# Folding the adaLN sums in place, and moving each unit's first scaling to ScalarE

## The chip, the core and the metric

The kernel runs on one core of a Trainium2 chip. It is measured by the device time of one execution in microseconds; lower is better. Five engines work side by side, each through its own queue in order, and wait for each other by semaphores: TensorE (PE; its weight loads are shown apart as PEld), VectorE (DVE), ScalarE (ACT), GpSimd (POOL) and SyncE (SP), which here only issues DMAs.

## The reference: what is computed

One inference step through two layers of a diffusion backbone on 384 tokens (128 of context, 256 latent). Each layer is a half-step SwiGLU FFN, a mixer of four head groups, and a second FFN. Every sub-layer's input is normalised and then scaled, shifted and gated by nine vectors that come from a conditioning vector:

```
mod_ctx = (jax.nn.silu(c_ctx) @ w_ada[l] + b_ada[l]).reshape(1, N_MOD, -1)
mod_lat = (jax.nn.silu(c) @ w_ada[l] + b_ada[l]).reshape(c.shape[0], N_MOD, -1)
h = rmsnorm(x, p['g_ff1']) * (1 + part(1)) + part(0)
x = x + 0.5 * part(2) * swiglu(h, p['w1_gate'], p['w1_up'], p['w1_down'])
```

`w_ada[l]` is 1024 x 9216, so for each layer the kernel has to multiply two vectors (context and latent) with a matrix of 36 MB. These two products are the adaLN sums.

## The kernel before, in words

**FFN.** The weights come in pieces of 128 x 1024 by SP's DMAs. Each piece is split in two: ScalarE rounds it to `hi` (L243), VectorE takes the rest as `lo` (L244), and TensorE makes three products of each block (L248 to L250), each with a 128x128 stationary block and 384 moving columns. The first half of an FFN (`gate_up`) makes the hidden rows `sg`, which ScalarE and VectorE finish (L567, L568) and split into `ah`, `al` (L253, L254); the second half multiplies them with the down weights into `pd`.

**The adaLN sums** run beside three of the four FFNs. The plan cuts the columns of `w_ada` that the start does not compute into 43 units (42 of three column tiles of 128, one of two). A unit (`ada_steps`) loads its 128 x 8 x 384 weights into `flat`. With the 1024 inputs as 8 groups `k` of 128 partitions, it builds for each of the two streams `s` a partial sum per partition in `acc[:, s, :]`: the first scaling writes it (L276), seven more add to it (L278, multiply and add). Then the sum over the 128 partitions is left, `ada_reduce`:

```
298  nc.gpsimd.dma_start(out=fold[0:64, :c], in_=acc[64:128, 0, :c])
299  nc.gpsimd.dma_start(out=fold[64:128, :c], in_=acc[0:64, 1, :c])
302  G.tensor_tensor(out=fold[h, :c], in0=acc[h, s, :c], in1=fold[h, :c], op=ALU.add)
308  T.transpose(pt[:, m * P:(m + 1) * P], fold[:, m * P:(m + 1) * P], ident)
310  S.activation(out=junk[:, 0:64], in_=pt[:, m * 64:(m + 1) * 64], func=AF.Identity, accum_out=pm[:, m:m + 1])
```

Two transfers fold one half of the partitions of each stream onto the other, two POOL additions add them, TensorE transposes the three tiles, and ScalarE sums the columns by six accumulating activations. `ada_finish` (L268, L269) adds the bias and multiplies by the gain into `mod`.

**What sets the order.** `Filler` gives the units out in steps. Each piece of an FFN's weights earns it a number of credits (`up(2 * ru)`, `dn(rd)`), at a rate of 8 steps a unit; one credit is one `k` of the unit at work. A finished unit's reduction is started at once (its transfers and POOL additions), and its TensorE part is given out six steps later (`late`, `flush`). Two units are loaded at a time, and `acc` has two buffers. Within this the framework's scheduler, which has a cost model of its own, sets each engine's order; the mixer's attention part is scheduled by hand and has no units.

Of the kernel before, what the change touches and what calls it, by code (L numbers as in the profile page):

```python
# [9 lines left out]
F32 = mybir.dt.float32  # L10
# [3 lines left out]
AF = mybir.ActivationFunctionType  # L14
ALU = mybir.AluOpType
AX = mybir.AxisListType

P = 128
DM = 1024
KD = DM // P  # L20
# [70 lines left out]
def trunk_kernel(ctx: ExitStack, tc: tile.TileContext, I: dict, C: dict, O: list):  # L91
    nc = tc.nc
    V, S, G, T = nc.vector, nc.scalar, nc.gpsimd, nc.tensor
# [7 lines left out]
    sm = ctx.enter_context(tc.tile_pool(name="sm", bufs=2))  # L101
# [7 lines left out]
    def small(name):  # L109
        return psm.tile([P, 512], F32, tag="sm", name=name)  # L110
# [4 lines left out]
    def cload(name, shape, src, pool=None, eng=None):  # L115
        t = (pool or const).tile(shape, F32, name=name)
        (eng or nc.gpsimd).dma_start(out=t, in_=src)
        return t
# [46 lines left out]
    ident = cload("ident", [P, P], C["ident"], eng=nc.scalar)  # L165
    cols_b0 = columns("b0", [("b_ada0", row128(I["b_ada"][0:1]), 72, nc.scalar), ("g_ff1", row128(I["g_ff1"]), 16, nc.scalar)])
    ones = const.tile([P, P], F32, name="ones")
    V.memset(ones, 1.0)
    sc = const.tile([P, KD, 2], F32, name="sc")
# [88 lines left out]
    junk = const.tile([P, P], F32, name="junk")  # L258
# [4 lines left out]
    def ada_load(w, l, kt, n):  # L263
        nc.sync.dma_start(out=w, in_=I["w_ada"][l][:, kt * P:(kt + n) * P].rearrange("(k p) f -> p k f", p=P))

    def ada_finish(l, kt, n, sums):
        mp = mod[:, l, kt:kt + n, :]
        V.tensor_tensor(out=mp, in0=sums.rearrange("p (k s) -> p k s", s=2), in1=bc(badd[:, l, kt:kt + n].unsqueeze(2), [P, n, 2]), op=ALU.add)  # L268
        V.tensor_tensor(out=mp, in0=mp, in1=bc(bmul[:, l, kt:kt + n].unsqueeze(2), [P, n, 2]), op=ALU.mult)  # L269

    last_step = [None]

    def ada_product(acc, w, n, k):
        for s in range(2):
            if k == 0:
                last_step[0] = V.tensor_scalar(out=acc[:, s, :n * P], in0=w[:, 0, :], scalar1=sc[:, 0, s:s + 1], scalar2=None, op0=ALU.mult)  # L276
            else:
                last_step[0] = V.scalar_tensor_tensor(out=acc[:, s, :n * P], in0=w[:, k, :], scalar=sc[:, k, s:s + 1], in1=acc[:, s, :n * P], op0=ALU.mult, op1=ALU.add)  # L278

    def ada_acc():  # L280
        return sm.tile([P, 2, 3 * P], F32, tag="adacc", bufs=2, name="adacc")
# [12 lines left out]

    def ada_reduce(acc, l, kt, n):
        c = n * P
        fold = sm.tile([P, 3 * P], F32, tag="adfold", bufs=1, name="adfold")
        nc.gpsimd.dma_start(out=fold[0:64, :c], in_=acc[64:128, 0, :c])  # L298
        nc.gpsimd.dma_start(out=fold[64:128, :c], in_=acc[0:64, 1, :c])
        for s in range(2):  # L300
            h = slice(64 * s, 64 * s + 64)
            G.tensor_tensor(out=fold[h, :c], in0=acc[h, s, :c], in1=fold[h, :c], op=ALU.add)  # L302

        yield False
        pm = sm.tile([P, 6], F32, tag="adasum", bufs=2, name="adasum")
        pt = small(f"ada{l}_{kt}")
        for m in range(n):
            T.transpose(pt[:, m * P:(m + 1) * P], fold[:, m * P:(m + 1) * P], ident)
        for m in range(2 * n):
            S.activation(out=junk[:, 0:64], in_=pt[:, m * 64:(m + 1) * 64], func=AF.Identity, accum_out=pm[:, m:m + 1])  # L310
        ada_finish(l, kt, n, pm[:, :2 * n])

    def ada_steps(l, kt, n, stage):

        w = stage(n)
        ada_load(w, l, kt, n)
        yield True
        acc = ada_acc()
        for k in range(KD):
            ada_product(acc, w, n, k)  # L320
            if k < KD - 1:
                yield True
        red = ada_reduce(acc, l, kt, n)
        next(red)
        yield red
# [12 lines left out]
    class Filler:  # L338
# [1 line left out]
        late = []  # L340

        def __init__(self, units, stage):
            self.units, self.stage, self.run, self.credit = list(units), stage, [], 0.0

        def start(self):
            if self.units:
                g = ada_steps(*self.units.pop(0), self.stage)
                next(g)
                self.run.append(g)

        def __call__(self, steps):
            self.credit += steps
            while self.credit >= 1.0 and (self.run or self.units):
                self.credit -= 1.0
                while len(self.run) < 2 and self.units:
                    self.start()
                red = next(self.run[0])
                if red is not True:
                    self.run.pop(0)
                    self.late.append([6, red])  # L360
                self.flush(1)

        def flush(self, steps):
            for t in list(self.late):
                t[0] -= steps
                if t[0] < 0:
                    self.late.remove(t)
                    with tc.issue_after(last_step[0].ins):
                        next(t[1], None)

        def begin(self):
            for _ in range(2):
# [1301 lines left out]
```

## Time and profile before

| | us |
|---|---|
| median of 3 runs | 1611.67 (1611.38 to 1614.06) |
| the profiled execution | 1614.9 |
| its span, first to last instruction | 1613.1 |
| PE busy | 1561.6 (97%) |
| DVE busy | 1245.8 (77%) |
| ACT busy | 786.8 (49%) |
| POOL busy | 255.4 (16%) |

A busy time is the sum of an engine's instructions. Products overlap in TensorE's pipeline: one lasts 0.34 us, while the next starts 0.17 us after it. What a product costs is therefore read from the distance of starts, and not from its length. An f32 product (not fp32r, as the FFN's are) is recorded as two passes, each with its own weight load, so three products show as x6.

### The profile page before, as it was taken

Reading aid. Unit: us, or ns where it says so; the run is one execution under the profiler, and the core shown is the slowest. Engines: PE = TensorE matmul, PEld = TensorE weight load, DVE = VectorE, ACT = ScalarE, POOL = GpSimd, SP = SyncE. Lnnn points to the kernel's source line nnn. Section 1 sums busy time; section 2 is a strip of 40 time slices with the busy share of each in tenths; the row PEclk is TensorE's granted clock in tenths of the full one; section 3 lists DMA queues with packets and bytes.
Section 4 is the critical chain, followed back from the end, with each engine's and each line's share of the span. In section 5 each row is a group of like instructions: output and inputs, shape, how many; then the busy total and the mean of one; then the engine's idle time right before and its main releaser. Section 6 shows DMA issues by size and latency. Waiting matters only on the chain. (4 is left out here: it accounts for less than half of the span.)

```text
span 1613.1 us, 24761 instructions
## 1 busy us (share of the span) xinstructions
PE 1561.6 (97%) x9027; PEld 1467.4 (91%) x9027; DVE 1245.8 (77%) x2485; ACT 786.8 (49%) x1838; POOL 255.4 (16%) x334
## 2 busy tenths in 40 slices
PE   7899999999999999999999999999999999999997
PEld 5789989997867999999999999999886799999997
DVE  5799997997878699996999977698787767434333
ACT  5544434548465554444546344454846656333332
POOL 2112221232040001131220212123004000000000
PEclk9999999999999999999999999999999999999999
DMA  9757758664432367867676865675344234444341
GB/s 309 247 151 232 225 185 247 208 199 120 121 75 75 109 204 232 253 179 222 212 206 192 250 195 164 213 231 158 116 111 86 66 110 126 122 126 131 118 137 46
DMA packets 233375, 270.68 MB, mean 168 GB/s; under 512 B 12392, under 2 KB 217936, under 8 KB 233253
## 3 DMA queue, kind: packets, MB, share of 16 engines
q1 hardware_dynamic: 223232, 248.67, 50.8%
q0 software_dynamic: 9744, 20.31, 5.3%
q8 instruction: 71, 1.16, 0.3%
q14 instruction: 52, 0.42, 0.1%
q10 hardware_dynamic: 276, 0.11, 0.0%
HBM read 257.10 MB, written 3.57 MB: 162 GB/s over the span
## 5 line engine op out<-in xcount | busy, mean ns | idle before, releaser
L278 DVE SCALAR_TENSOR_TENSOR adacc<-flat,sc,adacc 128x384 f32<-128x384 f32 (+1 forms) x602 | 357.2, 646 | 0.0
L302 POOL TENSOR_TENSOR adfold<-adacc,adfold 64x384 f32<-64x384 f32 (+1 forms) x86 | 118.0, 1372 | 174.7 <-DMA adfold<-adacc 172.3
L253 ACT CAST ah<-sg 128x384 fp32r<-128x384 f32 x88 | 45.1, 513 | 163.1 <-DVE sg L568 162.3
L250 PE MATMUL pd<-ah,lo_db 128*128 128x384 f32 x352 | 118.8, 338 | 1.6 <-DVE lo_db L244 1.4
L250 PE MATMUL pd<-ah,lo_da 128*128 128x384 f32 x352 | 118.7, 337 | 1.6 <-DVE lo_da L244 1.6
L249 PE MATMUL pg<-wide,hi_gb 128*128 128x384 f32 (+1 forms) x352 | 119.3, 339 | 0.2
L248 PE MATMUL pd<-ah,hi_da 128*128 128x384 f32 x352 | 119.3, 339 | 0.0
L248 PE MATMUL pg<-wide,hi_gb 128*128 128x384 f32 (+1 forms) x352 | 119.2, 339 | 0.0
L248 PE MATMUL pd<-ah,hi_db 128*128 128x384 f32 x352 | 118.9, 338 | 0.0
L250 PE MATMUL pg<-wide,lo_gb 128*128 128x384 f32 (+1 forms) x352 | 118.5, 337 | 0.0
L249 PE MATMUL pu<-wide,hi_ub 128*128 128x384 f32 (+1 forms) x352 | 118.4, 336 | 0.0
L249 PE MATMUL pd<-al,hi_db 128*128 128x384 f32 x352 | 118.4, 336 | 0.0
L249 PE MATMUL pd<-al,hi_da 128*128 128x384 f32 x352 | 118.4, 336 | 0.0
L248 PE MATMUL pu<-wide,hi_ub 128*128 128x384 f32 (+1 forms) x352 | 118.2, 337 | 0.0
L250 PE MATMUL pu<-wide,lo_ub 128*128 128x384 f32 (+1 forms) x352 | 117.8, 337 | 0.0
L248 PE MATMUL pu<-wide,hi_ua 128*128 128x384 f32 (+1 forms) x328 | 111.3, 340 | 4.2 <-DVE sg L568 4.2
L250 PE MATMUL pg<-wide,lo_ga 128*128 128x384 f32 (+1 forms) x328 | 112.0, 343 | 1.9 <-DVE lo_ga L244 1.9
L248 PE MATMUL pg<-wide,hi_ga 128*128 128x384 f32 (+1 forms) x328 | 113.5, 346 | 0.0
L249 PE MATMUL pg<-wide,hi_ga 128*128 128x384 f32 (+1 forms) x328 | 112.0, 342 | 0.0
L298 POOL DMA_DIRECT2D adfold<-adacc x43 | 23.9, 556 | 550.5 <-DVE adacc L278 352.0
L249 PE MATMUL pu<-wide,hi_ua 128*128 128x384 f32 (+1 forms) x328 | 110.9, 338 | 0.0
L250 PE MATMUL pu<-wide,lo_ua 128*128 128x384 f32 (+1 forms) x328 | 110.6, 338 | 0.0
(504 smaller groups left out, 4290.9 us busy)
## 6 DMA issues: line engine op xcount, KB each, us to landing
flat<-in_w_ada_dram SPq DMA_DIRECT2D x42, 1536.0 KB, 8.1
st_gb<-in_w_gate_dram SPq DMA_DIRECT2D x44, 512.0 KB, 3.8
st_ub<-in_w_up_dram SPq DMA_DIRECT2D x44, 512.0 KB, 4.5
st_ga<-in_w_gate_dram SPq DMA_DIRECT2D x41, 512.0 KB, 3.9
st_ua<-in_w_up_dram SPq DMA_DIRECT2D x41, 512.0 KB, 4.9
st_da<-in_w_down_dram SPq DMA_DIRECT2D x40, 512.0 KB, 4.8
st_db<-in_w_down_dram SPq DMA_DIRECT2D x40, 512.0 KB, 3.5
wst<-in_w_ada_dram SPq DMA_DIRECT2D x8, 1024.0 KB, 12.6
```

The lines of the kernel that those rows point to most:

```text
L248: T.matmul(out, lhsT=lh, rhs=rh, start=start, stop=False)
L249: T.matmul(out, lhsT=lh, rhs=rl, start=False, stop=False)
L250: T.matmul(out, lhsT=ll, rhs=rh, start=False, stop=stop)
L253: S.copy(hi, src)
L278: last_step[0] = V.scalar_tensor_tensor(out=acc[:, s, :n * P], in0=w[:, k, :], scalar=sc[:, k, s:s + 1], in1=acc[:, s, :n * P], op0=ALU.mu ...
L298: nc.gpsimd.dma_start(out=fold[0:64, :c], in_=acc[64:128, 0, :c])
L302: G.tensor_tensor(out=fold[h, :c], in0=acc[h, s, :c], in1=fold[h, :c], op=ALU.add)
```

## The change

Four things are done, and the order of instructions follows from them.

- The two fold transfers add into `acc` itself (`accum_op`), so that `acc[0:64, 0]` and `acc[64:128, 1]` hold what `fold` held. The POOL additions and `fold` go.
- The sum over the remaining 64 partitions is made by products with a column of ones: for each stream and each tile one f32 product with a 64x128 stationary block and one moving column, six a unit, in place of three transposes. Two small copies take the results, in place of six accumulating activations. `ada_finish` comes two steps later.
- The first scaling (`k = 0`) goes from VectorE to ScalarE.
- It is given out a step ahead, when the unit before is done (`primed`), so that a unit takes seven credits and not eight.

```
     def ada_product(acc, w, n, k):
         for s in range(2):
             if k == 0:
-                last_step[0] = V.tensor_scalar(out=acc[:, s, :n * P], in0=w[:, 0, :], scalar1=sc[:, 0, s:s + 1], scalar2=None, op0=ALU.mult)
+                S.activation(out=acc[:, s, :n * P], in_=w[:, 0, :], func=AF.Identity, scale=sc[:, 0, s:s + 1])
...
         c = n * P
-        fold = sm.tile([P, 3 * P], F32, tag="adfold", bufs=1, name="adfold")
-        nc.gpsimd.dma_start(out=fold[0:64, :c], in_=acc[64:128, 0, :c])
-        nc.gpsimd.dma_start(out=fold[64:128, :c], in_=acc[0:64, 1, :c])
+        nc.gpsimd.dma_start(out=acc[0:64, 0, :c], in_=acc[64:128, 0, :c], accum_op=ALU.add)
+        nc.gpsimd.dma_start(out=acc[64:128, 1, :c], in_=acc[0:64, 1, :c], accum_op=ALU.add)
+
+        yield 2
+        pm = sm.tile([P, 6], F32, tag="adasum", bufs=2, name="adasum")
         for s in range(2):
             h = slice(64 * s, 64 * s + 64)
-            G.tensor_tensor(out=fold[h, :c], in0=acc[h, s, :c], in1=fold[h, :c], op=ALU.add)
-
-        yield False
-        pm = sm.tile([P, 6], F32, tag="adasum", bufs=2, name="adasum")
-        pt = small(f"ada{l}_{kt}")
-        for m in range(n):
-            T.transpose(pt[:, m * P:(m + 1) * P], fold[:, m * P:(m + 1) * P], ident)
-        for m in range(2 * n):
-            S.activation(out=junk[:, 0:64], in_=pt[:, m * 64:(m + 1) * 64], func=AF.Identity, accum_out=pm[:, m:m + 1])
+            pt = small(f"ada{l}_{kt}")
+            for m in range(n):
+                T.matmul(pt[:, m:m + 1], lhsT=acc[h, s, m * P:(m + 1) * P], rhs=ones[h, 0:1], start=True, stop=True)
+            S.copy(pm[:, s:2 * n:2], pt[:, :n])
+        yield 2
         ada_finish(l, kt, n, pm[:, :2 * n])
...
                 while len(self.run) < 2 and self.units:
                     self.start()
+                if not self.primed:
+                    next(self.run[0])
+                    self.primed = True
                 red = next(self.run[0])
                 if red is not True:
                     self.run.pop(0)
                     self.late.append([6, red])
+                    self.primed = False
                 self.flush(1)
+
+                if not self.primed and self.run:
+                    next(self.run[0])
+                    self.primed = True
```

On TensorE, this is the place of one unit's reduction (`ada_25`, `ada_28`: layer 0, column tiles 25 and 28) in the first FFN, between two pieces of weights. Before:

```order
L248 MATMUL pu_1505<-wide_228,hi_ua_4_1602 128x384
L249 MATMUL pu_1505<-wide_229,hi_ua_4_1602 128x384
L250 MATMUL pu_1505<-wide_228,lo_ua_4_1603 128x384
L308 MATMUL ada_25_1720<-ident,adfold 128x128 x3
L248 MATMUL pg_1699<-wide_228,hi_ga_0_1705 128x384
L249 MATMUL pg_1699<-wide_229,hi_ga_0_1705 128x384
```

Three transposes stand there. In the changed kernel a like place reads:

```order
L248 MATMUL pu_1515<-wide_228,hi_ua_4_1603 128x384
L249 MATMUL pu_1515<-wide_229,hi_ua_4_1603 128x384
L250 MATMUL pu_1515<-wide_228,lo_ua_4_1604 128x384
L306 MATMUL ada_28_1744<-ones,adacc 128x1 x3
L306 MATMUL ada_28_1749<-ones,adacc 128x1 x3
L248 MATMUL pg_1717<-wide_228,hi_ga_0_1723 128x384
L249 MATMUL pg_1717<-wide_229,hi_ga_0_1723 128x384
```

The two streams' three products stand in a row, first those on partitions 0 to 63, then those on 64 to 127, with nothing between.

On ScalarE, around one reduction of the same FFN (`hi_` are the weights' roundings, `flat` a unit's weights, `sg` and `ah` hidden rows). Before:

```order
L310 ACTIVATE junk,adasum<-ada_25_1720 128x64
L253 CAST ah_673<-sg 128x384
L310 ACTIVATE junk,adasum<-ada_25_1720 128x64 x5
L243 CAST hi_ga_0_1878<-st_ga_0_1876 128x1024
L243 CAST hi_ua_0_1884<-st_ua_0_1882 128x1024
```

And in the changed kernel:

```order
L307 COPY adasum<-ada_28_1744 128x3
L307 COPY adasum<-ada_28_1749 128x3
L276 ACTIVATE adacc<-flat_1629,sc 128x384
L253 CAST ah_673<-sg 128x384
L276 ACTIVATE adacc<-flat_1629,sc 128x384
L243 CAST hi_ga_0_1895<-st_ga_0_1893 128x1024
L243 CAST hi_ua_0_1901<-st_ua_0_1899 128x1024
```

Six activations became two copies, and the first scalings of a coming unit stand right behind them, ahead of the next pieces' roundings.

## Rows read from the trace of the kernel before

**Rows 1.** the page: busy time, share of the span, instructions of each engine:

```profile
PE 1561.6 (97%) x9027; PEld 1467.4 (91%) x9027; DVE 1245.8 (77%) x2485; ACT 786.8 (49%) x1838; POOL 255.4 (16%) x334
```

**Rows 2.** stretches where units run: length, each engine's busy time, clock, DMA; their sum:

```profile
128.00:205.00 77.00, 77.00 (x444) 75.14 (x443) 76.90 (x127) 33.54 (x94) 22.34 (x23) 1.00 0.75 231
205.00:235.00 30.00, 26.58 (x155) 25.79 (x154) 30.00 (x52) 11.74 (x26) 5.13 (x7) 1.00 0.59 183
...
sum 832.00, PE 822.16 PEld 809.08 DVE 751.18 ACT 384.47 POOL 178.85; mean PE 117.45 PEld 115.58 DVE 107.31 ACT 54.92 POOL 25.55
```

**Rows 3.** waits of PE, whole run: us in total, times, longest:

```profile
PE pu L248 <- DVE sg L568: 4.2, 4, 2.1
```

**Rows 4.** groups by line: busy us, mean ns of one, idle before:

```profile
L278 DVE SCALAR_TENSOR_TENSOR adacc<-flat,sc,adacc 128x384 f32<-128x384 f32 (+1 forms) x602 | 357.2, 646 | 0.0
...
L302 POOL TENSOR_TENSOR adfold<-adacc,adfold 64x384 f32<-64x384 f32 (+1 forms) x86 | 118.0, 1372 | 174.7 <-DMA adfold<-adacc 172.3
...
L310 ACT ACTIVATE junk<-ada 128x64 f32<-128x64 f32 x256 | 56.8, 222 | 6.2
...
L310 ACT ACTIVATION_READ_ACCUMULATOR junk<-ada 128x1 f32 x256 | 49.8, 195 | 0.0
...
L276 DVE TENSOR_SCALAR adacc<-flat,sc 128x384 f32<-128x384 f32 (+1 forms) x86 | 33.3, 421 | 13.5 <-POOL adfold L302 12.2 <-DMA flat<-in_w_ada_dram 1.2
...
L395 ACT ACTIVATE sq<-xt 128x384 f32<-128x384 f32 x42 | 21.7, 517 | 40.2 <-DVE xt L464 40.1
...
L308 PE MATMUL ada<-ident,adfold 128*128 128x128 f32 x128 | 21.2, 273 | 0.0
```

**Rows 5.** timeline of PE around three transposes: start us, us, instruction:

```profile
168.36 0.34 PE L248 MATMUL pu<-wide,hi_ua 128*128 128x384 f32 x1
...
168.71 0.34 PE L250 MATMUL pu<-wide,lo_ua 128*128 128x384 f32 x1
168.88 0.49 PE L308 MATMUL ada<-ident,adfold 128*128 128x128 f32 x3
169.13 0.42 PE L248 MATMUL pg<-wide,hi_ga 128*128 128x384 f32 x1
169.39 0.34 PE L249 MATMUL pg<-wide,hi_ga 128*128 128x384 f32 x1
```

**Rows 6.** timeline of PE around three f32 products of one column:

```profile
358.19 0.34 PE L250 MATMUL pqk<-wide,lo_aqk 128*128 128x386 f32 x1
358.37 0.72 PE L416 MATMUL stm<-ones,accm 128*128 128x1 f32 x6
358.95 0.42 PE L248 MATMUL pqk<-wide,hi_aqk 128*128 128x386 f32 x1
359.21 0.34 PE L249 MATMUL pqk<-wide,hi_aqk 128*128 128x386 f32 x1
```

**Rows 7.** timeline of PE around f32 products on 64 rows, both halves:

```profile
472.41 0.33 PE L250 MATMUL pdu<-wide,lo_du 128*128 128x384 f32 x1
472.67 0.49 PE L1081 MATMUL s<-qT 64*128 64x128 f32 x4
473.10 0.66 PE L1117 MATMUL s<-ident,pe 128*128 128x128 f32 x4
```

**Rows 8.** timeline of PE, four f32 products, two on each half:

```profile
395.86 0.71 PE L907 MATMUL pP<-qk 64*128 64x128 f32 x8
396.51 0.44 PE L912 MATMUL pk<-ident,qk 128*128 128x128 f32 x2
```

**Rows 9.** line 1081's products, 384 and 128 columns: min, median, max ns:

```profile
L1081 PE MATMUL s<-qT x96: 271/482/588, 454.4 to 1276.6; 64*128 64x384 f32 x64, 64*128 64x128 f32 x32
```

**Rows 10.** timeline of POOL: a fold's first transfer is issued:

```profile
169.93 0.54 POOL L298 DMA_DIRECT2D adfold<-adacc  x1 [5.35 <-DVE adacc L278]
```

**Rows 11.** timeline of PE: the transposes of that fold:

```profile
185.86 0.49 PE L308 MATMUL ada<-ident,adfold 128*128 128x128 f32 x3
```

**Rows 12.** the fold's tile: how long its transfers take:

```profile
DMA to landing us min/median/max: 2.0/4.4/8.0
```

More of the change, by code (lines that the diff above doesn't have):

```diff
@@ L318, in ada_steps @@
         acc = ada_acc()
-        for k in range(KD):
+        ada_product(acc, w, n, 0)
+        yield True
+        for k in range(1, KD):
             ada_product(acc, w, n, k)
@@ L342, in __init__ @@
         def __init__(self, units, stage):
-            self.units, self.stage, self.run, self.credit = list(units), stage, [], 0.0
+            self.units, self.stage, self.run, self.credit, self.primed = list(units), stage, [], 0.0, False
         def start(self):
@@ L365, in flush @@
                 t[0] -= steps
-                if t[0] < 0:
-                    self.late.remove(t)
+                while t in self.late and t[0] < 0:
                     with tc.issue_after(last_step[0].ins):
-                        next(t[1], None)
+                        more = next(t[1], None)
+                    if more is None:
+                        self.late.remove(t)
+                    else:
+                        t[0] += more
         def begin(self):
```

## The prediction, made before the changed kernel was run

> **What bounds the kernel now.** I read the shares of busy time first. TensorE is busy for 97% of the span and VectorE, the next, for 77% [rows 1]. A mean may hide a stage in which another engine decides, so I took next the stretches in which the adaLN units run. The seven that I looked at make 832.00 us, and TensorE is busy for 822.16 of them, at a granted clock of 1.00 in the two shown [rows 2]. All that it stands idle there is 9.84 us. Its products follow each other at 0.17 to 0.18 us, the pace that the front names [rows 5]. So in these stages the end is set by the number of starts on TensorE, and what is put between two products there goes to the end nearly whole, while what goes away on other engines is worth at most the 9.84 us.
>
> One stretch shows a second limit. From 128 to 235 us VectorE is busy for 76.90 of 77 us and 30.00 of 30, and in its second part TensorE loses 3.42 us [rows 2]. The largest wait of TensorE on VectorE in the FFNs, for the hidden row `sg` that frees a PSUM bank, comes to 4.2 us in the whole run [rows 3].
>
> **The products with ones (TensorE).** First what goes: 128 transposes [rows 4], which is 42 units of three and one of two. From 168.36 to 168.71 two starts take 0.35 us; across three transposes, the second start after 168.71 is at 169.39, 0.68 us later [rows 5]. So three transposes cost 0.68 - 0.35 = 0.33 us, two of them 0.22 at 0.11 each.
>
> What comes is, for each unit of three, six f32 products on 64 rows, with two passes each: twelve passes. The trace has no such group, so I build it from three rows.
> - Going in: the FFN-like product at 472.41 is followed at 472.67 by the first on 64 rows, 0.26 us later in place of 0.17 [rows 7].
> - The passes: two products on 64 rows, one on each half of the partitions, are four passes, and take 0.43 us until the next product on 128 rows starts (472.67 to 473.10) [rows 7]. Four such products, the two of one half listed first and then the two of the other, are eight passes, and take 0.65 us (395.86 to 396.51) [rows 8]. Eight passes one after another at the 0.11 us per pass that a single half would need would be 0.9 us; so the halves run beside each other, and a pair of passes costs (0.65 - 0.43) / 2 = 0.11 us. The unit's two streams lie on the two halves, so its twelve passes are six pairs: 0.65 + 2 x 0.11 = 0.87 us. One moving column in place of 128 takes off the last pair's 127 columns: 384 columns last 482 ns and 128 last 271, 0.82 ns a column [rows 9], so 0.10 us. Left: 0.77 us.
> - Coming out: the first two products after a change start 0.26 us apart [rows 5, 6].
>
> A unit costs 0.26 + 0.77 + 0.26 - 0.35 = 0.94 us, so 0.94 - 0.33 = 0.61 more than now. The unit of two has four pairs, 0.72 - 0.22 = 0.50 more. Sum: 42 x 0.61 + 0.50 = 26.1 us, all of it on the path.
>
> The bounds. Below: six passes of one column on 128 rows, without any change of rows, cost 1.02 - 0.35 = 0.67 us (358.19 to 359.21) [rows 6]; if the halves overlap wholly and nothing drains, that is 0.34 more a unit, 14.5 in all. Above: if the second half waits for the first, six more passes of 0.11 us make 1.60 us, 1.27 more a unit and 42 x 1.27 + 0.94 = 54.3 in all. I take 26.1, since eight passes on two halves are the nearest row.
>
> On this place the Trainium skill speaks against my reading: "TensorE: Matmul & The Clock Gate", Part 3, says that matmuls start and end strictly in program order, and only weight loads are pulled ahead. By that rule the second stream's products cannot start before the first stream's last, and the sum would be the upper bound. The trace does not bear it out: the group of eight passes took 0.65 us, not 0.9 [rows 8].
>
> **The accumulating transfers and POOL.** 86 POOL additions of 1372 ns (118.0 us) go [rows 4]; POOL is busy for 16% [rows 1], so by itself this is worth nothing. They made VectorE wait for 12.2 us at the first scaling, and L278 takes 646 ns in the mean [rows 4]. The transfers stay two a unit. No row shows one that adds. A plain one lands in 4.4 us in the middle, 2.0 to 8.0 [rows 12], and reads only its source; one that adds has to read its target as well. Bounds: as long as now, or twice as long, 8.8 and at most 16.0. The cover: one fold was issued at 169.93 and its transposes started at 185.86 [rows 10, 11], 15.9 us, with the POOL additions in them, which go. So up to twice the time is hidden, and I take nothing; every microsecond beyond the cover would stall TensorE, up to 43 times.
>
> **The first scaling on ScalarE.** VectorE loses 86 x 421 ns, 33.3 us, ScalarE gets 86 of some 517 ns (L395 has their shape), 44 us, and loses the accumulating activations, 56.8 + 49.8 us [rows 4], against 86 small copies that cannot last longer than the scalings. ScalarE is busy for 49% [rows 1], so its sum is nothing. There is a new wait: the scaling needs an `acc` buffer, which now comes free only when TensorE has made the products of the unit before last, and the next weights' `hi` are queued behind it. But in the changed order the scalings stand directly behind the copies, and those wait for the same products, as the accumulating activations do now. The cover is the half of ScalarE's time that is free (33.54 of 77 us busy [rows 2]); if it were gone, two scalings of 0.52 us a unit would be late, 44 us.
>
> **Seven steps in place of eight.** VectorE's work for a step hardly changes: now (2 x 0.42 + 14 x 0.65) / 8 = 1.24 us, then 14 x 0.65 / 7 = 1.29 or less without POOL's additions. But the FFN's pieces between the steps get longer by the products with ones, so VectorE falls behind less, and the units end earlier. I give back the 3.42 us that TensorE loses between 205 and 235 us, where VectorE has no free time; bounds 0 and the 9.84 us of all seven stretches.
>
> **The sum.** 26.1 - 3.4 = +22.7 us. The profiled execution took 1614.9 us, so it would take 1637.6. It lies 3.2 us above the median of the runs, 1611.67, and against that the forecast is 1634.4.
>
> **Rivals.**
> - *The halves one after another.* +54.3 - 3.4 = +50.9, 1662.6 us. For it: each stream's three products stand together in the order, and six passes of one half lie ahead of the other half, where the trace shows four. Against it: the eight passes in 0.65 us [rows 8].
> - *No drain.* 14.5 - 3.4 = +11.1, 1622.8 us. For it: one column empties quickly. Against it: 0.26 us before and the late start behind 64-row products [rows 7].
> - *Faster: TensorE's new work costs no more than its old, and VectorE's relief decides.* It happens where the twelve passes and their changes cost under 0.33 us plus the idle time given back, 9.84 / 43 = 0.23, so under 0.56 us a unit. With passes as cheap as 0.025 us, twelve are 0.30, 0.03 less than the transposes, and the time is 1611.67 - 43 x 0.03 - 9.8 = 1600.6 us. Against it: one-column passes follow at 0.11 us (six between 358.37 and 358.95 [rows 6]). In the Trainium skill this is "TensorEngine Tiling", Instruction Overhead: a matmul costs some 60 cycles, whatever its free size is below that, which would be an estimate of 0.025 us at 2.4 GHz; the 0.11 us row contradicts it here, where each pass has its own weight load.
> - *The adding transfers come late.* From 15.9 us on they stall TensorE. At four times the usual 4.4 us, 17.6, each unit loses 1.7 us: 43 x 1.7 = 73 more than the forecast, 1707 us. Against it: the bytes are 96 KB a transfer as before.
>
> **How the numbers follow.** The forecast has 0.62, the halves in turn 0.14, no drain 0.11, faster 0.08, late transfers 0.05. The range takes in the first three: from no drain with all idle time given back (1611.67 + 14.5 - 9.8 = 1616.4) to the halves in turn with nothing given back, 1611.67 + 54.3 = 1666.0. All that is within 0.2% (3.2 us) counts as no change that a measurement can tell. That or better needs the faster rival, or no drain with more given back: 0.07 faster, 0.06 the same, 0.87 slower.
>
> **What would show it.** Right: around each `L306` the second start after the last product before it comes some 0.94 + 0.35 us later, with the pairs of passes starting together; TensorE's idle time between 128 and 235 us gone; each stage with units longer by 0.6 us a unit; mixers and the last FFN as now. Wrong: twelve starts 0.11 us apart in a line; TensorE waiting for the fold transfers; ScalarE's `hi` late behind a scaling that waits for TensorE; or starts so close that a unit costs under 0.56 us.

## The result, and the profile after

The changed kernel takes 1639.53 us (median; 1637.38 to 1641.23), the kernel before in the same session 1612.87 us. The ratio is 1.018, with an interval of 1.016 to 1.020: slower by 26.7 us. The profiled execution took 1637.38 us. The forecast was 1634.4 us, 22.7 above before. Two of its terms were wrong by some ten microseconds each, in opposite directions, as the runs below show, so that the forecast came so near is in part luck.

The first part of the page, to be read beside [rows 1]:

```profile
PE 1592.1 (97%) x9411; PEld 1494.1 (91%) x9411; DVE 1177.4 (72%) x2399; ACT 771.4 (47%) x1498; POOL 161.1 (10%) x248
```

TensorE has 384 instructions and 30.5 us of busy time more. All other engines have less to do, and the kernel is slower. The stretches of [rows 2], now (length, busy time of each engine, clock, DMA):

```profile
128.00:205.00 77.00, 76.91 (x463) 74.18 (x462) 66.92 (x116) 31.29 (x54) 11.64 (x15) 1.00 0.83 240
205.00:235.00 30.00, 30.00 (x189) 29.45 (x188) 26.17 (x46) 11.76 (x23) 3.27 (x4) 1.00 0.61 173
```

VectorE is no longer full there, and TensorE stands still nowhere between 205 and 235 us, where it lost 3.42 us. From the first to the last product of the FFN lines, the two stretches with units last 359.1 and 718.5 us in the trace, against 354.7 and 696.2 us: 26.7 us more. (That this is also the difference of the medians is chance: the spans of these two executions differ by 22.2 us, mainly since the mixer parts behind the stretches were 7.2 us shorter. The last FFN, which has no units, takes 277.3 us in both.) The groups that answer to [rows 4] (busy, mean ns of one, idle before it):

```profile
L278 DVE SCALAR_TENSOR_TENSOR adacc<-flat,sc,adacc 128x384 f32<-128x384 f32 (+1 forms) x602 | 335.2, 608 | 4.8 <-ACT adacc L276 4.7
...
L276 ACT ACTIVATE adacc<-flat,sc 128x384 f32<-128x384 f32 (+1 forms) x86 | 48.7, 610 | 9.3 <-DMA flat<-in_w_ada_dram 9.3
...
L306 PE MATMUL ada<-ones,adacc 64*128 64x1 f32 x512 | 46.3, 250 | 0.1
```

TensorE has waited only 0.1 us in all ahead of the products with ones: the adding transfers are in time. They land later than the plain ones of [rows 12], 6.8 us against 4.4 in the middle:

```profile
DMA to landing us min/median/max: 2.5/6.8/9.3
```

One place shows the scaling on ScalarE at its worst. At 64 us it has waited 2.89 us for its weights, with a cast (`hi_ga`) behind it, and TensorE then waits 4.3 us for the rest `lo_ga`, which VectorE makes from `hi_ga`. ScalarE's timeline, then TensorE's wait in this kernel and the same wait in the kernel before (us in total, times, longest):

```profile
64.35 1.12 ACT L276 ACTIVATE adacc<-flat,sc 128x384 f32<-128x384 f32 x2 [2.89 <-DMA flat<-in_w_ada_dram]
65.38 1.48 ACT L1486 ACTIVATE wide<-nt,mod 128x128 fp32r<-128x128 f32 x4
66.76 1.03 ACT L243 CAST hi_ga<-st_ga 128x1024 fp32r<-128x1024 f32 x1
```

```profile
PE pg L250 <- DVE lo_ga L244: 4.3, 1, 4.3
```

```profile
PE pg L250 <- DVE lo_ga L244: 1.9, 1, 1.9
```

So this place costs some 2.4 us more. The three runs below that have the scaling on VectorE show 1.9 to 2.0 us there too.

What the products cost is read as in [rows 5]: from the last FFN product ahead of them to the second one behind them. TensorE's timeline around a unit of three (start, us, instruction):

```profile
158.92 0.34 PE L250 MATMUL pu<-wide,lo_ua 128*128 128x384 f32 x1
159.19 1.08 PE L306 MATMUL ada<-ones,adacc 64*128 64x1 f32 x12
160.19 0.44 PE L248 MATMUL pg<-wide,hi_ga 128*128 128x384 f32 x1
160.47 0.34 PE L249 MATMUL pg<-wide,hi_ga 128*128 128x384 f32 x1
```

160.47 - 158.92 = 1.55 us, less the 0.35 us that two starts take anyway: the group puts the FFN off by 1.20 us (1.21 from the unrounded starts, the same in all 37 groups that stand between FFN products), where 0.94 was forecast. The unit of two has eight passes:

```profile
647.61 0.34 PE L250 MATMUL pu<-wide,lo_ub 128*128 128x384 f32 x1
647.88 0.62 PE L306 MATMUL ada<-ones,adacc 64*128 64x1 f32 x8
648.42 0.44 PE L248 MATMUL pg<-wide,hi_gb 128*128 128x384 f32 x1
648.71 0.34 PE L249 MATMUL pg<-wide,hi_gb 128*128 128x384 f32 x1
```

It costs 1.10 - 0.35 = 0.75 us. Call 0.11 us, the distance from one pass to the next, a place; two passes that run as a pair share one. Four passes less save 0.46 us, four places, where pairs would save two. So some passes of one stream do not run beside the other stream's. The starts say which. Line 306 in the first 0.25 us of either group (number of starts behind the x):

```profile
L306 PEld LDWEIGHTS ada<-ones,adacc x3: 183/186/188, 159.2 to 159.4; 64*128 64x128 f32 x3
...
L306 PEld LDWEIGHTS ada<-ones,adacc x6: 183/186/188, 647.9 to 648.1; 64*128 64x128 f32 x6
```

With four passes of the first stream ahead of it, the second stream starts beside the first, 0.01 us after it. With six ahead, three weight loads start alone in this time; the second stream's first product starts 0.25 us after the first's, just behind the third of the six. So two passes at the start and two at the end have no partner: eight places for twelve passes.

### The profile page after: what moved, and what is told of

Same layout as the page of the kernel before. It is cut to its first block, busy times and chain, and to the rows that moved or that the text cites. A ratio compares the mean times of both kernels' runs of the same rounds, so it can differ in the third digit from the quotient of the medians.

```text
span 1635.3 us, 25138 instructions
## 1 busy us (share of the span) xinstructions
PE 1592.1 (97%) x9411; PEld 1494.1 (91%) x9411; DVE 1177.4 (72%) x2399; ACT 771.4 (47%) x1498; POOL 161.1 (10%) x248
## 3 DMA queue, kind: packets, MB, share of 16 engines
q8 instruction: 74, 1.21, 0.3%
## 4 chain that ended last, share of the span: by engine, by line
PE 85%; DVE 6%; issue 3%; ACT 3%; DMA 3%; POOL 0%; ACTq 0%; SPq 0%; DVEq 0%; POOLq 0%
PE pg L248 7%; PE pg L250 7%; PE pg L249 7%; PE pu L250 7%; PE pu L249 7%; PE pu L248 7%; PE pd L248 7%; PE pd L250 7%; PE pd L249 7%; PE ada L306 2%; PE pwo L248 1%; DVE adacc L278 1%; PE pwo L249 1%; PE pwo L250 1%; DMA flat<-in_w_ada_dram 1%
## 5 line engine op out<-in xcount | busy, mean ns | idle before, releaser
L278 DVE SCALAR_TENSOR_TENSOR adacc<-flat,sc,adacc 128x384 f32<-128x384 f32 (+1 forms) x602 | 335.2, 608 | 4.8 <-ACT adacc L276 4.7
L297 POOL DMA_DIRECT2D adacc<-adacc x43 | 35.1, 817 | 753.4 <-issue 358.7
L244 DVE TENSOR_TENSOR lo_db<-st_db,hi_db 128x1024 fp32r<-128x1024 f32 (+1 forms) x48 | 53.8, 1133 | 64.5 <-ACT hi_db L243 64.5
L244 DVE TENSOR_TENSOR lo_gb<-st_gb,hi_gb 128x1024 fp32r<-128x1024 f32 x44 | 53.8, 1223 | 62.2 <-ACT hi_gb L243 62.1
```

Source lines behind the costliest of these rows:

```text
L244: V.tensor_tensor(out=lo[:, :n], in0=st[:, :n], in1=hi[:, :n].bitcast(F32), op=ALU.subtract)]
L297: nc.gpsimd.dma_start(out=acc[0:64, 0, :c], in_=acc[64:128, 0, :c], accum_op=ALU.add)
```

## Experiments

Ratios are to the kernel before, timed on the same chip between the runs. 0.001 is 1.6 us.

**Where TensorE's time goes: the order of the six products.**

```
-        for s in range(2):
...
-            for m in range(n):
-                T.matmul(pt[:, m:m + 1], lhsT=acc[h, s, m * P:(m + 1) * P], rhs=ones[h, 0:1], start=True, stop=True)
...
+        for m in range(n):
+            for s in range(2):
...
+                T.matmul(pt[s][:, m:m + 1], lhsT=acc[h, s, m * P:(m + 1) * P], rhs=ones[h, 0:1], start=True, stop=True)
```

> Only the order of a unit's six products is changed: one of the first stream, one of the second, and so on, each stream in its own PSUM bank. In the trace of the changed kernel the second stream's first pass starts 0.25 us after the first stream's, and the twelve passes take eight places of 0.11 us; in the unit of two, with four passes ahead, it starts 0.013 us after. Theory A (TensorE looks only some four passes ahead, so the order holds the second half back): all twelve go in pairs, six places, the group puts off the products by 1.21 - 0.22 = 0.99 us, and the time is 1639.5 - 43 x 0.22 = 1630 us. Theory B (the second half is late for its PSUM bank or its semaphore, or pairs of f32 passes are slower here than in the mixer): no change, 1639.5 us.

Measured: 1628.85 us, ratio 1.0114 (1.0096 to 1.0133). TensorE's timeline in this kernel:

```profile
158.25 0.34 PE L250 MATMUL pu<-wide,lo_ua 128*128 128x384 f32 x1
158.52 0.83 PE L306 MATMUL ada<-ones,adacc 64*128 64x1 f32 x12
159.29 0.45 PE L248 MATMUL pg<-wide,hi_ga 128*128 128x384 f32 x1
159.57 0.34 PE L249 MATMUL pg<-wide,hi_ga 128*128 128x384 f32 x1
```

1.32 - 0.35 = 0.97 us a unit: six places, and 10.7 us less than the changed kernel, where theory A had 9.5.

The second order lists two of the first stream, two of the second, then one of each:

```
+        for ms in (range(min(2, n)), range(2, n)):
+            for s in range(2):
...
+                for m in ms:
+                    T.matmul(pt[s][:, m:m + 1], lhsT=acc[h, s, m * P:(m + 1) * P], rhs=ones[h, 0:1], start=True, stop=True)
```

> Only the order of a unit's six products is changed: two of the first stream, two of the second, then one of each. Theory A (TensorE holds some four passes ahead of the one that runs, so a half is held back only by passes of the other half beyond the fourth): all passes go in pairs as in the order by turns, and the group puts off the FFN's products by 0.97 us, 1629 us in all. Theory B (each change of half in the list costs, and only strict turns pair): between 0.97 and 1.21 us, near 1.1, 1634 us.

Measured: 1627.88 us (one run, without an interval). Its timeline:

```profile
159.32 0.34 PE L250 MATMUL pu<-wide,lo_ua 128*128 128x384 f32 x1
159.59 0.84 PE L307 MATMUL ada<-ones,adacc 64*128 64x1 f32 x12
160.36 0.45 PE L248 MATMUL pg<-wide,hi_ga 128*128 128x384 f32 x1
160.65 0.34 PE L249 MATMUL pg<-wide,hi_ga 128*128 128x384 f32 x1
```

1.33 - 0.35 = 0.98 us. Four passes of one half ahead of the other hold nothing back, six do. The three prices fit one sum: 0.75, 0.97 and 1.21 us for four, six and eight places are 0.11 a place and 0.31 to 0.33 for going to 64 rows and back.

**Without the change of rows.** ScalarE copies the folded halves into one tile of 128 rows (two copies), and three products with a two-column matrix sum both streams.

```
+        S.copy(fold[0:64, :c], acc[0:64, 0, :c])
+        S.copy(fold[64:128, :c], acc[64:128, 1, :c])
...
+            T.matmul(pt[:, 2 * m:2 * m + 2], lhsT=fold[:, m * P:(m + 1) * P], rhs=sel, start=True, stop=True)
```

> The folded halves are copied by ScalarE into one tile of 128 rows, and the sums are three f32 products on all 128 rows with a matrix of two columns (ones above, ones below): six passes and no change between 64 and 128 rows. The transfers and the first scaling stay as changed. Theory A (no drain at a change of rows, six passes as in the rows of before, 0.67 us a unit instead of 1.21): 1639.5 - 43 x 0.54 = 1616 us. Theory B (a small product costs its place in line whatever its rows, and the drain is there all the same): six passes in place of eight places, 1639.5 - 43 x 0.22 = 1630 us. ScalarE gets some 39 us of copies more, which both put at nothing.

Measured: 1624.97 us, ratio 1.0099 (1.0078 to 1.0121). Around one group:

```profile
163.68 0.34 PE L254 MATMUL pu<-wide,lo_ua 128*128 128x384 f32 x1
163.85 0.72 PE L312 MATMUL ada<-sel,adfold 128*128 128x2 f32 x6
164.44 0.42 PE L252 MATMUL pg<-wide,hi_ga 128*128 128x384 f32 x1
164.69 0.34 PE L253 MATMUL pg<-wide,hi_ga 128*128 128x384 f32 x1
```

The group costs 0.67 us in 37 of 37 places between FFN products, as the prediction's lower bound had it [rows 6]: six passes on 128 rows take six places and next to nothing more, so the 0.31 to 0.33 us above belong to the 64 rows. The time fell by 14.6 us, where this price alone would give 23. What took the rest no run shows by itself; ScalarE's copies wait in line for the transfers (us in total, times, longest):

```profile
ACT adfold L306 <- DMA adacc<-adacc: 57.6, 16, 7.0
...
ACT adfold L307 <- DMA adacc<-adacc: 23.8, 20, 3.2
```

**The old sums in the new order.** Two runs with three transposes a unit; the first with the fold and POOL's additions of before (shown), the second with the adding transfers and, in place of the additions, ScalarE's two copies.

```
-                T.matmul(pt[:, m:m + 1], lhsT=acc[h, s, m * P:(m + 1) * P], rhs=ones[h, 0:1], start=True, stop=True)
...
+            G.tensor_tensor(out=fold[h, :c], in0=acc[h, s, :c], in1=fold[h, :c], op=ALU.add)
...
+            T.transpose(pt[:, m * P:(m + 1) * P], fold[:, m * P:(m + 1) * P], ident)
```

> The products with ones and the adding transfers are undone: fold tile, plain transfers, two additions on POOL, three transposes, accumulating activations, as in the kernel before. The first scaling on ScalarE and the seven steps stay. By the starts in the trace a unit's twelve passes put off the FFN's products by 1.21 us, the three transposes by 0.335. Theory A (the passes cost 0.87 us a unit more, and the rest of the change takes some 10 us of waits from TensorE): 1639.5 - 43 x 0.87 = 1602 us, 10 below the kernel before. Theory B (the prediction's sizes: 0.61 us a unit, 3.4 us given back): 1612.9 - 3.4 = 1609.5 us. If the waits went away because POOL's additions went, they are back here, and the time is that of the kernel before, 1613 us.

> The adding transfers and the first scaling on ScalarE stay as changed; the folded halves are copied by ScalarE into one tile, which three transposes and six accumulating activations sum, as in the kernel before. So POOL adds nothing, and TensorE pays 0.335 us a unit. Theory A (all that the change cost are the products, and what it gives back comes from VectorE free of POOL): 1639.5 - 43 x 0.87 = 1602 us, at or below the run with the additions on POOL. Theory B (what is given back comes from the first scaling on ScalarE alone): the same as the run with the additions on POOL. If ScalarE's copies, which stand ahead of the casts of the weights and wait for the transfers, cost TensorE something, it is slower than that run, 1605 to 1613 us.

Measured: 1649.16 us (ratio 1.0246, 1.0226 to 1.0266) and 1648.99 us (1.0241, 1.022 to 1.0262). No theory named these times: the transposes cost 0.335 us as before, and yet both kernels are slower than the changed one. (The two are equal, as theory B of the second had it, but both far above the times that it allowed for, and with different waits.) The waits of ScalarE in the first, and of ScalarE and TensorE in the second:

```profile
ACT adacc L276 <- POOL adfold L302: 86.9, 18, 9.5
...
ACT adacc L276 <- DMA flat<-in_w_ada_dram: 41.7, 16, 7.0
```

```profile
ACT adfold L302 <- DMA adacc<-adacc: 41.6, 14, 8.7
...
ACT adfold L303 <- DMA adacc<-adacc: 34.9, 20, 4.4
...
PE pg L248 <- ACT sg L580: 6.5, 3, 5.5
```

ScalarE is busy for 50% in the first of these kernels, and yet TensorE starves: in ScalarE's line the scaling (or the copy) waits for POOL or a transfer, and the FFN's own `sg` and casts stand behind it. That this is the cause is tested by the next run. The stretch around one such wait in the second kernel (busy of PE, PEld, DVE, ACT, POOL; then clock):

```profile
636.00:643.00 7.00, 7.00 (x43) 7.00 (x42) 7.00 (x13) 0.32 (x3) 1.64 (x2) 1.00 0.94 251
643.00:647.00 4.00, 0.84 (x5) 0.52 (x4) 0.92 (x3) 0.72 (x3) 0.00 (x0) 0.97 1.07 341
647.00:654.00 7.00, 4.67 (x16) 4.67 (x17) 4.14 (x12) 5.26 (x16) 0.93 (x2) 0.53 0.35 111
```

A copy waits 8.7 us for its transfer, until 645 us, and from 643 us on TensorE, VectorE and ScalarE nearly stand still; then the granted clock is 0.53, about the lower of its two levels, for 7 us, and 16 products start where 43 did.

**The copy on POOL.** So that nothing on ScalarE waits for a transfer, POOL copies one folded half into the other stream's tile:

```
+        nc.gpsimd.tensor_copy(out=acc[64:128, 0, :c], in_=acc[64:128, 1, :c])
...
+            T.transpose(pt[:, m * P:(m + 1) * P], acc[:, 0, m * P:(m + 1) * P], ident)
```

> As the run with ScalarE's copies and transposes, but the folded second half is copied behind the transfers by POOL (one copy of 64 rows a unit) into the other half of the first stream's tile, and three transposes and six accumulating activations sum it. So nothing on ScalarE waits for a transfer or for POOL: the next scaling waits for TensorE's transposes, as in the changed kernel. Theory A (what made the two runs with transposes slow were the waits of 87 and 76 us that stood ahead of the casts in ScalarE's queue): they are gone, TensorE pays 0.335 in place of 1.21 us a unit, and the time is 1639.5 - 43 x 0.87 = 1602 us, or some us more for 43 copies on POOL beside VectorE. Theory B (ScalarE cannot carry both the scalings and the accumulating activations, whatever waits): as slow as those two, 1649 us.

Measured: 1624.1 us, ratio 1.0075 (1.0053 to 1.0096): 25 us better than the two runs before it, so theory B fell, and taking those waits out of ScalarE's line gave that much back; but 22 us short of theory A. Its POOL, shortly ahead of TensorE's longest wait for it (4.9 us; start, us, instruction, idle before):

```profile
127.05 0.56 POOL L724 DMA_DIRECT2D Hd<-H  x1 [3.82 <-DVE adacc L278]
127.60 0.88 POOL L297 DMA_DIRECT2D adacc<-adacc  x1
128.15 1.18 POOL L298 DMA_DIRECT2D adacc<-adacc  x1
135.90 3.69 POOL L299 COPY adacc<-adacc 64x384 f32<-64x384 f32 x1 [6.57 <-DMA adacc<-adacc]
```

From the first issue to the end of the copy pass 12.0 us, and here, with seven steps a unit, the transposes are due at 134.7 us, 4.9 us before that. Two kernels leave work out of this one, the transfers with POOL's copy, and the accumulating activations:

> The run with transposes and POOL's copy came out at 1624 us where 1602 was expected. Here its two transfers and POOL's copy are left out (the transposes read the unfolded tile of the first stream, so the sums are not those of the reference); all else stays. Theory A (the transfers land late: landing and POOL's copy stall TensorE or hold back buffers): what it lost comes back, about 1602 us. Theory B (ScalarE is the one that is late, with scalings and accumulating activations together): only the 8 us that TensorE waited for POOL come back, 1616 us or more.

> The run with transposes and POOL's copy, its six accumulating activations a unit replaced by one small copy (the transposed columns are not summed, so the result is not the reference's): ScalarE gets rid of 106 us. Theory A (the transfers land late): no change, about 1620 us. Theory B (ScalarE is late with scalings and accumulating activations together, and the products with ones paid for themselves in part by taking the latter away): 1602 to 1610 us.

Measured: 1603.1 us (0.9937, 0.992 to 0.9954) and 1616.86 us (1.0024, 1.0007 to 1.0042). Leaving out the transfers and the copy gives the missing 22 us back within 1 us. Only 8.1 of them are waits of TensorE for POOL, in two places; by which waits the others pass on is open. The accumulating activations are worth some 7 us here as well; since the first gain is already the whole, the two overlap.

**The scaling back on VectorE**, in the changed kernel:

```
-                S.activation(out=acc[:, s, :n * P], in_=w[:, 0, :], func=AF.Identity, scale=sc[:, 0, s:s + 1])
+                last_step[0] = V.tensor_scalar(out=acc[:, s, :n * P], in0=w[:, 0, :], scalar1=sc[:, 0, s:s + 1], ...
```

> The changed kernel with the first scaling back on VectorE, given out at the same place; transfers, products with ones and steps stay. VectorE gets 86 x 0.42 = 36 us more, and its scaling now waits for TensorE's products of the unit before last, with everything else of VectorE queued behind it. Theory A (the waits that TensorE lost, some 12 us, went because VectorE lost the scalings): 1639.5 + 12 = 1651 us or more. Theory B (they went because POOL's additions no longer slow VectorE): about 1639.5 us, with L278 still at 608 ns.

Measured: 1646.46 us, ratio 1.0223 (1.0203 to 1.0243), between the two theories. L278 stays at 606 ns. VectorE waits in line for TensorE:

```profile
L276 DVE TENSOR_SCALAR adacc<-flat,sc 128x384 f32<-128x384 f32 (+1 forms) x86 | 32.3, 412 | 11.5 <-PE ada L306 10.1 <-DMA flat<-in_w_ada_dram 1.3
```

**The parts in the old order.** Here the scheduling of before stays (eight steps, nothing given out ahead). First the fold by adding transfers and POOL's copy, scaling on VectorE and transposes as before; then the same with the products with ones; then the first of them with the scaling on ScalarE.

> The kernel before, its fold made by the two adding transfers and one copy on POOL in place of two additions; first scaling on VectorE, eight steps and transposes as before. VectorE's scaling now waits for the transposes of the unit before last. Theory A (POOL's additions beside VectorE are what cost the kernel before its waits): L278 goes from 646 to some 610 ns, and 3 to 10 us are given back, 1603 to 1610 us. Theory B (VectorE waiting in line for TensorE, 10 us in the run with the scaling on VectorE, costs as much as it wins): 1611 to 1620 us.

> The kernel before with two parts of the change alone: the adding transfers and the products with ones (in the listed order of the change). First scaling on VectorE and eight steps as before. It differs from the fastest run (1601.9 us, adding transfers, POOL's copy and transposes in the order of before) in little but the sums. Theory A (all of the products' 1.21 - 0.335 = 0.87 us a unit lies on the path): 1602 + 43 x 0.87 = 1639 us, no less than the whole change, whose scaling on ScalarE and seven steps then bring nothing in sum. Theory B (TensorE's longer stages hide other waits, or 43 copies less on POOL and 106 us less on ScalarE give time back): 1615 to 1630 us.

> The fastest run (1601.9 us) with the first scaling on ScalarE at its own step, eight steps as before. Theory A (ScalarE has half its time free, and VectorE loses 36 us): 1595 to 1602 us, as the scaling on ScalarE was worth 7 us in the changed kernel. Theory B (in ScalarE's queue the scaling waits for the transposes of the unit before last, with casts behind it, and VectorE's second scaling waits for ScalarE): slower, 1605 to 1620 us.

Measured: 1601.87 us (0.9925, 0.9902 to 0.9948); 1635.55 us (1.0141, 1.0121 to 1.0161); 1599.34 us (0.9917, 0.99 to 0.9935). The first and the last beat both kernels, and their intervals overlap. From the first to the second the products with ones cost 0.0216, 35 us: theory A but for 3 us. (POOL's copies and ScalarE's accumulating activations go in the same step; what they are worth here no run shows.) In the first, the groups that answer to [rows 4], with POOL's copies:

```profile
L278 DVE SCALAR_TENSOR_TENSOR adacc<-flat,sc,adacc 128x384 f32<-128x384 f32 (+1 forms) x602 | 341.3, 614 | 0.0
...
L299 POOL COPY adacc<-adacc 64x384 f32<-64x384 f32 (+1 forms) x43 | 49.4, 1150 | 232.0 <-DMA adacc<-adacc 231.9
...
L276 DVE TENSOR_SCALAR adacc<-flat,sc 128x384 f32<-128x384 f32 (+1 forms) x86 | 32.4, 412 | 6.6 <-PE ada L305 2.9 <-DMA flat<-in_w_ada_dram 1.7 <-POOL adacc L299 1.1
```

L278 falls from 646 to 614 ns in the mean, and VectorE's wait for POOL from 12.2 to 1.1 us. The middle one of the L278 never changed. Shortest, middle and longest in the kernel before and in the changed one (the shapes at a line's end are counted over a part of the 602):

```profile
L278 DVE SCALAR_TENSOR_TENSOR adacc<-flat,sc,adacc x602: 472/612/1398, 73.2 to 1103.7; 128x384 f32<-128x384 f32 x147, 128x256 f32<-128x256 f32 x4
```

```profile
L278 DVE SCALAR_TENSOR_TENSOR adacc<-flat,sc,adacc x602: 477/611/622, 74.7 to 1128.6; 128x384 f32<-128x384 f32 x147, 128x256 f32<-128x256 f32 x4
```

By start and end in the trace of before, 63 of the 602 ran beside a POOL addition and took 960 ns in the mean; the other 539 took 609, none over 628. Beside the copies of the run above it is 59, with 704 ns. In 205 to 235 us VectorE now has time to spare in that run (27.04 of 30):

```profile
205.00:235.00 30.00, 28.70 (x169) 28.34 (x168) 27.04 (x49) 13.11 (x37) 9.82 (x7) 1.00 0.72 211
```

## Why the prediction came out as it did

Along one path through these runs the change is made up of three differences of ratios: POOL's additions replaced, 0.9925 - 1 = -0.0075 (-12 us); the products with ones, +0.0216 (+35 us); the scaling on ScalarE with seven steps, 1.018 - 1.0141 = +0.004 (+6 us, with intervals that just meet, so perhaps nothing). The third splits further: seven steps +0.0082 (+13 us, 1.0141 to 1.0223), then the scaling on ScalarE -0.0043 (-7 us). Together +29 us by ratios, 27 by the medians.

- *TensorE bounds, and what is put there goes to the end.* Right. By starts the products cost 42 x 0.87 + 0.5 = 37 us more than the transposes; 35 arrive, some 5 us either way by the intervals. Taking 0.24 us a unit away by order alone gave back 10.7 us where 9.5 were expected. One part was too low: relief on other engines was to be worth at most the 9.84 us in which TensorE stands idle, and replacing the additions alone gave 12. TensorE counts as busy at the lower clock as well: between 100 and 125 us it was granted 0.86 in the kernel before, 1.00 in the changed kernel and in the run with POOL's additions replaced.
- *"So its twelve passes are six pairs."* This step failed: from the first pass to the next FFN product it is 1.00 us (159.19 to 160.19), where 0.77 stood, so 0.87 us a unit more than the transposes where 0.61 stood, 11 us too few. The row behind it [rows 8] has four passes of a half ahead of the other; I carried it to six. The forecast of 0.94 us holds for the orders by turns and by twos (0.97 and 0.98). The rival of halves in turn listed this very point in its favour, but put the price at 1.60 us; 1.21 lies between. The faster rival needed less than 0.56. The rule of the Trainium skill that I weighed ("TensorE: Matmul & The Clock Gate", Part 3: matmuls start strictly in program order) is not borne out: in the listed order the second stream's first product starts 0.25 us after the first stream's, whose six passes need 5 x 0.11 = 0.55 us to the start of the last.
- *Going in and out, 0.26 each.* Right: 0.27 us in (158.92 to 159.19) and 0.28 out (160.19 to 160.47).
- *The accumulating transfers hidden.* Right in the changed kernel (6.8 us, 1.5 times the plain ones, inside the bound of twice). It does not hold in every order: with seven steps and transposes, they and POOL's copy cost 21 us (1624.1 against 1603.1).
- *POOL's additions, "by itself this is worth nothing".* Failed, by 12 us: the L278 beside the additions took 960 ns where the others took 609, and the first scaling waited for POOL. I had both numbers, the mean of 646 ns and the wait of 12.2 us, and credited only TensorE's idle time in one stretch. The mean is 646 and 647 ns in the two kernels with additions, 612 to 618 in the four with copies, 606 to 616 in those with neither. How much of the 12 us is the longer L278, and how much the wait or the single `fold` buffer, which went with the additions, no run takes apart.
- *The scaling on ScalarE, 0.* Right in the old order, where TensorE's transposes free its buffer: -0.0008, within the intervals. In the new order it gave 7 us (-0.0043). (Its 33.3 us are VectorE's busy time; 86 x 421 ns would be 36.2, since overlaps count once in a busy time.) The cover that I named was the wrong one. ScalarE had half its time free in the two runs that lost 39 us as well (0.0246 and 0.0241); what matters is what a scaling waits for, and what stands behind it.
- *Seven steps, a relief of 3.4 us.* Failed. The stall from 205 to 235 us went, but it goes as well with eight steps: 1.30 us of 3.42 are left in the run with POOL's copy, none in the one with the products with ones (TensorE busy for 30.00 of 30 us). And seven steps, with what is given out ahead, cost time in both pairs of runs that differ in little else (in the second also in `ada_finish`, two steps later). With the scaling on ScalarE, POOL's copy and transposes, eight steps give 1599.3 us and seven 1624.1; with the products with ones and the scaling on VectorE 1.0141 and 1.0223. In the changed kernel itself they were not tried alone.

So 9 to 11 us too few for the products and about 9 too few for the relief cancelled, and the rest is the 6 us of scaling and steps. That those two cancelled is luck; the forecast was near for half a reason.

## What to carry to other kernels

A group of small products is priced by its order too: list the two row halves by turns, or by at most two f32 products each, and look at a row with as many passes ahead as the new code has. Free time of an engine hides work, not a wait in its line: ask of each instruction that is moved what it waits for and what stands behind it. Look at the longest of a group and not only at its mean: here VectorE paid for what POOL added beside it, in one L278 of ten, and taking the additions away (adding transfers, one copy) was the part of this change that gained.

## What the runs showed that I had not expected

A long stall costs twice. After the 4 us in which TensorE was busy for 0.84 us it was granted the lower clock for some 7 us, and the run with POOL's copy shows the same behind its 4.9 us (0.74 of 4 us, then a clock of 0.51 for 7 us); over the whole first run the mean clock is 0.980, against 0.993 in the changed kernel. And one copy of 64 rows on POOL took 3.69 us beside VectorE, where the mean of 43 in that run is 1.23.
